# The diagonal of the recurrences' score tiles: from GpSimd's selects to VectorE's predicated copies

## The chip, the cores and the metric

One core of a Trainium2 chip runs the whole kernel. Its engines are TensorE (PE, and PEld for its weight loads), VectorE (DVE), ScalarE (ACT), GpSimd (POOL) and SyncE (SP, which issues most DMAs). The metric is the device time of one execution in microseconds (us): the median of three runs of the kernel before is 814.64 us (814.58 to 815.78).

## The reference

One layer: an input projection of x (1024 tokens by 1024 channels), three causal mixers side by side, a gated sum of their three up-projections, an output projection and a layer norm.

```
proj = x @ w_in
y_a  = stick-breaking attention(a_q, a_k, a_v) * silu(a_g)            # 4 heads
y_b  = rmsnorm(recurrence(h_q, h_key, h_i, log_f)) * silu(h_g)        # HGRN2: 4 heads, key width 64
y_c  = rmsnorm(recurrence(c_q, c_k, c_v, c_log_f)) * silu(c_g)        # GLA: 4 heads, key width 32
out  = layer_norm(alpha * x + (sum_n sigmoid(gate_n) * (y_n @ w_up[n])) @ w_out)

recurrence:  S_t = diag(f_t) S_(t-1) + k_t^T v_t ;  o_t = S_t^T q_t
```

In chunks, o_t has a part from the state in front of the chunk and a part `scores @ v` inside the chunk, where `scores[t, s] = sum_k q[t,k] * exp(cum[t,k] - cum[s,k]) * k[s,k]` for s <= t and 0 elsewhere. On the diagonal (s = t) the decay is 1, so the entry is q_t . k_t.

## The kernel before

TensorE is given the projections as a stream of generators (`stream`): each takes 128 or 256 columns of w_in, splits them into a rounded part and a rest (ScalarE's `copy` and VectorE's `subtract` in `split`, lines 98 and 99) and runs three matmuls per product. Five chains are woven into that stream: two of attention (`c_sb`), then three recurrences (`c_rec`): GLA with four heads at once (`nh == 4`), and HGRN2 twice with two heads each, called H0 and H1 below. A `yield` in a chain gives its time budget to the stream. A scheduler then places the instructions on each engine's queue; a queue runs in order.

`c_rec` treats windows of 128 tokens. Its score tiles `sc` are 128 by 1024 float32: four in GLA, two in H0, two in H1 (`nbank`). They, and GLA's query tiles `Qbd`, lie in six shared buffers (`S`, `NSLOT = 6`), which the attention's transposed weights `ath` and `atl` use before. In order:

1. Matmuls of products q*k with a block of ones (line 826) give `r`: per token, window and head the diagonal q_t . k_t in the first half and the neighbour's entry, `r1`, in the second (VectorE copies it out of PSUM on line 827).
2. GpSimd sets `Qbd` and `Qlo` to zero, and makes each `sc` by an `affine_select` (line 843): `r` on the diagonal, zero elsewhere.
3. The levels h = 1, 2, 4, ..., 64. From h = 2 on, `scores` copies blocks of Q to `Qbd` (ScalarE, line 857), in GLA GpSimd takes the rounding rest to `Qlo` (line 860, eight instructions for half a level), TensorE multiplies with K (line 876), and the result goes to blocks of `sc`: by VectorE's `copy_predicated` (line 885) up to h = 16, by ScalarE from h = 32 (lines 883 and 880). Then Q and K are multiplied by the decays G (lines 899 and 900, VectorE) and G is halved (line 902, GpSimd).
4. `neighbours` (line 850): VectorE copies `r1` to every second element of `sc` under a mask, one instruction of 128x512 per tile.
5. The transposes of K (line 912), the states: matmuls to PSUM (line 929, two buffers) and a serial chain on VectorE (lines 935 and 937); then the outputs (lines 949 and 951, which read `sc`).

Of the kernel before, what the change touches and what calls it, by code (L numbers as in the profile page):

```python
# [10 lines left out]
I32 = mybir.dt.int32  # L11
AF = mybir.ActivationFunctionType
ALU = mybir.AluOpType
# [3 lines left out]
P = 128  # L17
# [38 lines left out]
def hybrid_layer_kernel(ctx, tc, x, x_t, w_in, gla_gate_w2, gla_gate_b, hgrn_lb_logits,  # L56
                        hgrn_norm_g, gla_norm_g, w_up, w_out, ln_g, ln_b, out):
    nc = tc.nc
# [10 lines left out]
    def nm(s):  # L69
        cnt[0] += 1  # L70
        return f"{s}_{cnt[0]}"

    def S(name, dt=F32, shape=None):
        return sp.tile(shape or [P, 1024], dt, tag="s", name=nm(name), bufs=NS)
# [71 lines left out]
    ident = const.tile([P, P], F32, name="ident")  # L146
# [666 lines left out]
    def c_rec(key, nh, V):  # L813

        G, K, Q, pr = d[key]
        wpb = 8 // nh
# [4 lines left out]
        r = sm.tile([P, 16 * nh], F32, tag="r", name=nm("r"))  # L821
# [7 lines left out]
        sc = [S("sc", shape=[P, wpb, nh, P]) for _ in range(nbank)]  # L829
# [9 lines left out]
                nc.gpsimd.memset(q.bitcast(F32), 0.0)  # L839
            Khi, Klo = [[R("Kp", F32R) for _ in range(2)] for _ in range(2)]  # L840
        for b in range(nbank):
            rb = r[:, b * wpb * nh:(b + 1) * wpb * nh]
            nc.gpsimd.affine_select(sc[b].rearrange("p w h t -> p (w h) t"), rb.unsqueeze(2).broadcast_to([P, wpb * nh, P]),
                                    [[0, wpb * nh], [-1, P]], compare_op=ALU.is_equal, fill=0.0, base=0, channel_multiplier=1)
        yield R0_T if nh == 4 else R02_T
        def neighbours():

            for b in range(nbank):
                dst = sc[b].rearrange("p w a (n two) -> p (w a) n two", two=2)[:, :, :, 1]
                nc.vector.copy_predicated(dst, masks[1].bitcast(I32)[:, :, 0].unsqueeze(1).broadcast_to([P, wpb * nh, 64]),  # L850
                                          r1[:, b * wpb * nh:(b + 1) * wpb * nh].unsqueeze(2).broadcast_to([P, wpb * nh, 64]))
# [37 lines left out]
        for h in LEVELS:  # L889
            nb = 64 // h  # L890
            for hf in range(2):
# [11 lines left out]
                G[hf] = Gn  # L903
                yield R4_T if nh == 4 else R2_T
        neighbours()

        kn = []
# [35 lines left out]
        for b in range(nbank):  # L943
            pt = pav([P, wpb, nh, 64])
            for wi in range(wpb):
                w = b * wpb + wi
# [67 lines left out]
    def og_h(tt):  # L1014
        return [(d["og", ("H", un)][tt // 4][:, tt % 4].rearrange("p a v -> p (a v)"), P, un * P) for un in range(2)]

    chains = [(("qk", 0), lambda: c_sb(0)), (("qk", 1), lambda: c_sb(1)),
              ("GLA", lambda: c_rec("GLA", 4, lambda w: d["vC"][w // 2][:, w % 2, :])),
              (("H", 0), lambda: c_rec(("H", 0), 2, lambda w: d["vH"][0][w // 4][:, w % 4, :])),
              (("H", 1), lambda: c_rec(("H", 1), 2, lambda w: d["vH"][1][w // 4][:, w % 4, :]))]  # L1020
    for label, mk in chains:
        need(label)
# [22 lines left out]
    for tq in range(4):  # L1045
# [5 lines left out]
        for t2 in range(2):  # L1051
            tt = tq * 2 + t2
            np_ = 4 if tt == 7 else 2
            w = D // np_
# [4 lines left out]
            for i, cs in enumerate(cols):  # L1059
# [3 lines left out]
                for k in range(8):  # L1063
                    a, b = mh[k // 2][:, k % 2, t2 * P:(t2 + 1) * P], ml[k // 2][:, k % 2, t2 * P:(t2 + 1) * P]
# [69 lines left out]
```

## Time and profile before

| | before |
|---|---|
| median of 3 runs | 814.64 us |
| the profiled execution, whole | 814.49 us |
| its span, first to last instruction | 812.8 us |
| PE busy, DVE busy | 795.8 us (98%), 573.0 us (71%) |
| ACT busy, POOL busy | 369.3 us (45%), 183.3 us (23%) |
| mean granted TensorE clock | 0.997 of full |

Matmuls are pipelined, so a busy share of 98% does not mean that TensorE is at its peak; a wait in front of a matmul shows as idle time. The rows further down give the start of an instruction or of a run of equal ones (us from the span's start), its length in us, engine, line, operation, what it writes and reads, how many there are, and in brackets the idle time of its engine before it with what ended that.

### The profile page before, as it was taken

How to read it: one execution, taken by the hardware profiler on the slowest of the kernel's cores; microseconds unless marked ns; L12 is line 12 of the kernel's file. 1: busy time of each engine (PE TensorE's matmuls, PEld its weight loads, DVE VectorE, ACT ScalarE, POOL GpSimd, SP SyncE). 2: the span in 40 equal slices, each digit the busy share in tenths (PEclk: the TensorE clock that was granted, in tenths of full speed). 3: DMA queues.
4: the chain of work that ended last, by engine and by line, in shares of the span. 5: the costliest groups of instructions: out<-in, count | busy, mean ns of one | idle time of the engine just before them, and what ended most of it. 6: DMA issues, size and time to landing. Idle time of an engine off the chain costs nothing.

```text
span 812.8 us, 12525 instructions
## 1 busy us (share of the span) xinstructions
PE 795.8 (98%) x4504; PEld 681.0 (84%) x4504; DVE 573.0 (71%) x1058; ACT 369.3 (45%) x777; POOL 183.3 (23%) x358
## 2 busy tenths in 40 slices
PE   8999999999999999999999999999999999999996
PEld 6988799787779989988888889888888878888886
DVE  6449897869965497678665964766658566686675
ACT  6456565696644737454655433332224223341110
POOL 4012213122587822212110002112113121100000
PEclk9999999999999999999999999999999999999998
DMA  9533110111011111010111120220122202532221
GB/s 268 145 84 79 27 27 2 45 31 30 24 35 34 53 27 28 22 44 20 34 33 33 40 63 3 66 65 16 55 59 66 61 12 84 194 105 103 105 102 54
DMA packets 67790, 48.33 MB, mean 59 GB/s; under 512 B 4608, under 2 KB 61584, under 8 KB 67728
## 3 DMA queue, kind: packets, MB, share of 16 engines
q1 hardware_dynamic: 66288, 44.46, 19.8%
q10 hardware_dynamic: 1440, 3.08, 1.0%
q8 instruction: 35, 0.57, 0.3%
q14 instruction: 27, 0.22, 0.1%
HBM read 41.23 MB, written 4.19 MB: 56 GB/s over the span
## 4 chain that ended last, share of the span: by engine, by line
PE 80%; DVE 9%; POOL 4%; issue 3%; ACT 2%; DMA 1%; SPq 0%; POOLq 0%; DVEq 0%; ACTq 0%
PE mm L207 18%; PE mm L220 13%; PE z L621 13%; PE mm L1066 11%; PE tr L621 7%; PE mm L621 5%; PE z L876 4%; PE mm L504 2%; POOL Qlo L860 2%; DVE om L751 2%; PE av L951 1%; PE av L789 1%; DVE be L752 1%; PE tr L767 1%; DVE atl L99 1%
## 5 line engine op out<-in xcount | busy, mean ns | idle before, releaser
L207 PE MATMUL mm<-xh,wh 128*128 128x512 f32 x320 | 130.2, 407 | 0.0
L207 PE MATMUL mm<-xh,wl 128*128 128x512 f32 x320 | 127.0, 397 | 0.0
L207 PE MATMUL mm<-xl,wh 128*128 128x512 f32 x320 | 126.6, 396 | 0.0
L99 DVE TENSOR_TENSOR wl<-wr,wh 128x512 fp32r<-128x512 f32 (+3 forms) x116 | 80.7, 705 | 47.3 <-PE z L621 22.5
L98 ACT CAST wh<-wr 128x512 fp32r<-128x512 f32 (+3 forms) x116 | 64.6, 568 | 76.2 <-PE mm L207 33.4
L220 PE MATMUL mm<-wh,xh 128*128 128x256 f32 (+1 forms) x320 | 92.0, 288 | 0.3 <-ACT wh L98 0.2
L220 PE MATMUL mm<-wl,xh 128*128 128x256 f32 (+1 forms) x320 | 91.1, 285 | 0.5 <-DVE wl L99 0.4
L220 PE MATMUL mm<-wh,xl 128*128 128x256 f32 (+1 forms) x320 | 90.6, 283 | 0.1
L1066 PE MATMUL mm<-wo,mh 128*128 128x512 f32 (+1 forms) x288 | 80.7, 366 | 0.0
L207 PEld LDWEIGHTS mm<-xh,wl 128*128 128x128 f32 x320 | 60.1, 188 | 13.4
L207 PEld LDWEIGHTS mm<-xh,wh 128*128 128x128 f32 x320 | 60.7, 190 | 11.8 <-DVE mT L507 0.5
L207 PEld LDWEIGHTS mm<-xl,wh 128*128 128x128 f32 x320 | 60.5, 189 | 11.0
L220 PEld LDWEIGHTS mm<-wh,xh 128*128 128x128 f32 x320 | 60.5, 189 | 1.6 <-ACT wh L98 1.4
L220 PEld LDWEIGHTS mm<-wl,xh 128*128 128x128 f32 x320 | 60.4, 189 | 1.1 <-DVE wl L99 1.1
L220 PEld LDWEIGHTS mm<-wh,xl 128*128 128x128 f32 x320 | 60.5, 189 | 0.4 <-DVE xl L99 0.3
L1066 PEld LDWEIGHTS mm<-wo,mh 128*128 128x128 f32 x288 | 52.1, 189 | 8.7
L1066 PE MATMUL mm<-wo,ml 128*128 128x512 f32 (+1 forms) x144 | 52.8, 367 | 0.0
L860 POOL TENSOR_TENSOR Qlo<-Q,Qbd 32x128 fp32r<-32x128 f32 x96 | 48.2, 519 | 2.6
L747 POOL TENSOR_SCALAR_AFFINE_SELECT om<-om 128x128 f32<-128x128 f32 x32 | 12.7, 398 | 138.8 <-ACT om L742 133.3
L621 PE MATMUL mm<-yh,wu 128*128 128x512 f32 x128 | 42.4, 393 | 0.0
L621 PE MATMUL z<-xh,wh 128*128 128x512 f32 x104 | 41.7, 401 | 0.0
L621 PE MATMUL z<-xh,wl 128*128 128x512 f32 x104 | 41.2, 396 | 0.0
(258 smaller groups left out, 1808.6 us busy)
## 6 DMA issues: line engine op xcount, KB each, us to landing
wr<-in_w_in_dram SPq DMA_DIRECT2D x92, 256.0 KB, 3.1
xraw<-in_x_t_dram SPq DMA_DIRECT2D x16, 256.0 KB, 5.6
wr<-in_w_out_dram SPq DMA_DIRECT2D x16, 256.0 KB, 3.0
xr<-in_x_dram SPq DMA_DIRECT2D x8, 512.0 KB, 3.4
wr<-in_w_up_dram SPq DMA_DIRECT2D x24, 128.0 KB, 2.2
out_dram<-xr SPq DMA_DIRECT2D x7, 256.0 KB, 2.1
out_dram<-xr ACTq DMA_DIRECT2D x7, 256.0 KB, 2.0
ks<-ks SPq DMA_DIRECT2D x8, 128.0 KB, 2.2
```

Source lines behind the costliest of these rows:

```text
L98: nc.scalar.copy(hi, src)
L99: nc.vector.tensor_tensor(lo, src, hi.bitcast(F32), op=ALU.subtract)
L207: mm(pt, w_, x_, start=(n == 0), stop=(n == 23))
L220: mm(pt, x_, w_, start=(n == 0), stop=(n == 23))
L504: mm(pu, w_, y_[th], start=(k == 0), stop=(k == 5))
L621: mm(pt, w_, x_, start=(start and i == 0), stop=(stop and i == len(ops) - 1), skip_group_check=True)
L747: nc.gpsimd.affine_select(a_[:, cw - P:cw], a_[:, cw - P:cw], [[-1, P]], compare_op=ALU.is_gt, fill=fill, base=0, channel_multiplier=1)
L751: nc.vector.tensor_tensor_scan(rv, rv, rv, 1.0 if last else rt[:, 0:1], op0=ALU.mult, op1=ALU.bypass)
L752: nc.vector.tensor_tensor(be[:, 0:cw - 1], be[:, 0:cw - 1], om[:, 1:cw], op=ALU.mult)
L860: nc.gpsimd.tensor_tensor(Qlo[hf][i][rr, a, :].rearrange("p (n h) -> p n h", h=h), qo[rr, i * nb * 2:i * nb * 2 + nb * 2], Qbd[hf].bitcast ...
L876: mm(pt[:, wi * nh:(wi + 1) * nh], k_[:, w * P:(w + 1) * P], q.rearrange("p a (n h) -> p a n h", h=h), start=(n == 0 and wi == 0), stop=(n ...
L1066: mm(pt, l_, r_[e][:, o:o + w], start=(n == 0), stop=(n == 23))
```

## The change

`affine_select` from `r` becomes a `memset` to zero that reads nothing, at the same place. The diagonal is put in by a new `copy_predicated` in `neighbours`, in front of the old one: the mask is the 128x128 identity (its bits are non-zero on the diagonal), repeated for each window and head, the data is `r`, repeated along the row, and the target is the whole tile, 128x1024. There is one for each of the eight tiles.

```diff
         for b in range(nbank):
-            rb = r[:, b * wpb * nh:(b + 1) * wpb * nh]
-            nc.gpsimd.affine_select(sc[b].rearrange("p w h t -> p (w h) t"), rb.unsqueeze(2).broadcast_to([P, wpb * nh, P]),
-                                    [[0, wpb * nh], [-1, P]], compare_op=ALU.is_equal, fill=0.0, base=0, channel_multiplier=1)
+            nc.gpsimd.memset(sc[b], 0.0)
         yield R0_T if nh == 4 else R02_T
         def neighbours():
 
             for b in range(nbank):
+                n_ = wpb * nh
+                nc.vector.copy_predicated(sc[b].rearrange("p w h t -> p (w h) t"), ident.bitcast(I32).unsqueeze(1).broadcast_to([P, n_, P]),
+                                          r[:, b * n_:(b + 1) * n_].unsqueeze(2).broadcast_to([P, n_, P]))
                 dst = sc[b].rearrange("p w a (n two) -> p (w a) n two", two=2)[:, :, :, 1]
```

Lines behind the edit move by one (the old copy is on line 851 after it, 936 and 938 are the state's chain). GpSimd's queue at the start of GLA's recurrence, with the semaphores that each instruction waits for; `sc_2634` to `sc_2637` are the four score tiles. Before:

```order
L843 AFFINE_SELECT sc_2634<-r_2583 128x1024 [waits DVE_49,Activation_49]
L843 AFFINE_SELECT sc_2635<-r_2583 128x1024 [waits PE_49]
L839 MEMSET Qlo_2642 128x512
L839 MEMSET Qlo_2643 128x512
L839 MEMSET Qlo_2644 128x512
L839 MEMSET Qlo_2645 128x512
L843 AFFINE_SELECT sc_2636<-r_2583 128x1024 [waits PE_49,Activation_49]
L843 AFFINE_SELECT sc_2637<-r_2583 128x1024 [waits PE_49]
L860 TENSOR_TENSOR Qlo_2642<-Q_2356,Qbd_2638 32x128 [waits Activation_49,Pool_49]
```

And after:

```order
L842 MEMSET sc_2634 128x1024 [waits DVE_49,PE_49]
L842 MEMSET sc_2635 128x1024 [waits PE_49]
L842 MEMSET sc_2636 128x1024 [waits DVE_49,PE_49]
L839 MEMSET Qlo_2642 128x512
L839 MEMSET Qlo_2643 128x512
L839 MEMSET Qlo_2644 128x512
L839 MEMSET Qlo_2645 128x512
L842 MEMSET sc_2637 128x1024 [waits PE_49]
L861 TENSOR_TENSOR Qlo_2642<-Q_2356,Qbd_2638 32x128 [waits Activation_49,Pool_49]
```

The third tile's instruction moved ahead of the memsets of `Qlo`; its wait for PE is for the attention's last matmuls (line 789), which read that buffer. In H0 and H1 the memsets moved up on GpSimd's queue to the end of GLA's recurrence, ahead of the memsets of `Qbd`.

VectorE's queue at the end of GLA's levels: from the last step on K (line 900) to the state's chain (`St`); the lines 421 to 423 and 99 are work for the stream. Before:

```order
L900 TENSOR_TENSOR K_2175<-K_2175,G_3467 128x4x64
L421 SCALAR_TENSOR_TENSOR e_3489<-s_594_3487,s_595_3488 128x512
L850 COPY_PREDICATED sc_2634<-mask_78,r_2583 128x512
L422 SCALAR_TENSOR_TENSOR s_594_3487<-e_3489,lb,s_594_3487 128x512
L423 TENSOR_SCALAR s_595_3488<-s_595_3488,lb_126 128x512
L850 COPY_PREDICATED sc_2635<-mask_78,r_2583 128x512
L99 TENSOR_TENSOR wl_3811<-wr_3808,wh_3810 128x512
L850 COPY_PREDICATED sc_2636<-mask_78,r_2583 128x512
L850 COPY_PREDICATED sc_2637<-mask_78,r_2583 128x512
L99 TENSOR_TENSOR wl_3817<-wr_3814,wh_3816 128x512
```

And after, to the same point:

```order
L421 SCALAR_TENSOR_TENSOR e_3489<-s_594_3487,s_595_3488 128x512
L848 COPY_PREDICATED sc_2634<-ident,r_2583 128x1024
L422 SCALAR_TENSOR_TENSOR s_594_3487<-e_3489,lb,s_594_3487 128x512
L423 TENSOR_SCALAR s_595_3488<-s_595_3488,lb_126 128x512
L851 COPY_PREDICATED sc_2634<-mask_78,r_2583 128x512
L848 COPY_PREDICATED sc_2635<-ident,r_2583 128x1024
L99 TENSOR_TENSOR wl_3815<-wr_3812,wh_3814 128x512
L851 COPY_PREDICATED sc_2635<-mask_78,r_2583 128x512
L848 COPY_PREDICATED sc_2636<-ident,r_2583 128x1024
L848 COPY_PREDICATED sc_2637<-ident,r_2583 128x1024
L99 TENSOR_TENSOR wl_3821<-wr_3818,wh_3820 128x512
L851 COPY_PREDICATED sc_2636<-mask_78,r_2583 128x512
```

Four new copies stand among the old ones; behind these rows come, in both, lines 421 to 423 once more and then the state's chain (after the change with the last old copy among them).

VectorE's queue at the end of H0's levels, from the last step on the first half of K (`s_595`) to the state's chain. Before:

```order
L850 COPY_PREDICATED sc_3925<-mask_78,r_3874 128x512
L900 TENSOR_TENSOR s_605_3589<-s_605_3589,G_4395 128x4x64
L850 COPY_PREDICATED sc_3926<-mask_78,r_3874 128x512
L433 TENSOR_TENSOR Q_4476<-mm_4427,s_718_4294 128x512
L434 TENSOR_TENSOR prod_4477<-mm_4427,s_719_4295 128x512
L116 TENSOR_TENSOR prod_4484<-Q_4476,s_719_4295 128x256
L899 TENSOR_TENSOR Q_4476<-Q_4476,s_718_4294 128x256
L104 TENSOR_TENSOR prod_4477<-prod_4477,prod_4421 128x512
L900 TENSOR_TENSOR s_719_4295<-s_719_4295,s_718_4294 128x256
L935 COPY St_4516<-z_4520 64x64
L106 TENSOR_TENSOR prod_4423<-prod_4477,prod_4421 128x512
L104 TENSOR_TENSOR prod_4484<-prod_4484,prod_4424 128x256
```

And after:

```order
L848 COPY_PREDICATED sc_3929<-ident,r_3878 128x1024
L851 COPY_PREDICATED sc_3929<-mask_78,r_3878 128x512
L901 TENSOR_TENSOR s_605_3589<-s_605_3589,G_4399 128x4x64
L848 COPY_PREDICATED sc_3930<-ident,r_3878 128x1024
L433 TENSOR_TENSOR Q_4480<-mm_4431,s_718_4298 128x512
L434 TENSOR_TENSOR prod_4481<-mm_4431,s_719_4299 128x512
L116 TENSOR_TENSOR prod_4488<-Q_4480,s_719_4299 128x256
L851 COPY_PREDICATED sc_3930<-mask_78,r_3878 128x512
L104 TENSOR_TENSOR prod_4481<-prod_4481,prod_4425 128x512
L900 TENSOR_TENSOR Q_4480<-Q_4480,s_718_4298 128x256
L936 COPY St_4522<-z_4526 64x64 x2
L938 SCALAR_TENSOR_TENSOR St_4522<-St_4522,G_4454,z_4526 64x64
```

Two copies came in, and the state's two first copies now stand ahead of lines 106, 104 and the step on `s_719`. TensorE's queue is the same but for two matmuls of the stream that stand a few places earlier behind H0's states.

## Rows read from the trace of the kernel before

**Rows 1.** TensorE's waits: for whom, total us, times, longest
```profile
PE av L789 <- DVE atl L99: 3.2, 4, 1.4
PE z L876 <- DVE sc L885: 1.0, 3, 0.7
```

**Rows 2.** VectorE's waits
```profile
DVE Q L899 <- POOL Qlo L860: 25.5, 12, 2.7
```

**Rows 3.** Timeline, start of GLA's recurrence: start, us, engine, line, [idle before]
```profile
206.24 1.85 POOL L834 MEMSET Qbd<- 128x1024 f32 x2 [7.36 <-PE av L789]
...
214.11 2.65 POOL L843 TENSOR_SCALAR_AFFINE_SELECT sc<-r 128x1024 f32<-128x1024 f32 x2 [6.03 <-ACT Qbd L857]
...
215.46 0.28 PE L789 MATMUL av<-atl,V 128*128 128x256 f32 x1
...
215.73 1.30 DVE L899 TENSOR_TENSOR Q<-Q,f 128x256 f32<-128x256 f32 x1
...
216.71 1.92 POOL L839 MEMSET Qlo<- 128x512 f32 x4
...
216.96 0.41 DVE L900 TENSOR_TENSOR K<-K,f 128x256 f32<-128x256 f32 x1
...
218.59 2.61 POOL L843 TENSOR_SCALAR_AFFINE_SELECT sc<-r 128x1024 f32<-128x1024 f32 x2
...
221.17 9.66 POOL L860 TENSOR_TENSOR Qlo<-Q,Qbd 32x128 fp32r<-32x128 f32 x16
```

**Rows 4.** Timeline, GLA's level h = 2
```profile
231.65 2.45 DVE L885 COPY_PREDICATED sc<-mask,z 128x512 f32<-128x512 int32 x2
...
232.99 0.74 PE L876 MATMUL z<-Qbd,Kp 128*128 128x256 f32 x4 [0.66 <-DVE sc L885]
```

**Rows 5.** Timeline, GLA's level h = 16
```profile
267.81 1.34 DVE L885 COPY_PREDICATED sc<-mask,z 128x512 f32<-128x512 int32 x2
```

**Rows 6.** Timeline, end of GLA's levels and its states
```profile
284.77 1.33 DVE L850 COPY_PREDICATED sc<-mask,r 128x512 f32<-128x512 int32 x1
...
289.11 2.48 DVE L850 COPY_PREDICATED sc<-mask,r 128x512 f32<-128x512 int32 x2
...
293.40 0.48 DVE L423 TENSOR_SCALAR s<-s,lb 128x512 f32<-128x512 f32 x1
...
293.84 0.97 DVE L935 COPY St<-z 32x64 f32<-32x64 f32 x4
...
294.85 7.39 DVE L937 SCALAR_TENSOR_TENSOR St<-St,G,z 32x64 f32<-32x64 f32 x24
...
295.59 0.40 PE L207 MATMUL mm<-xh,wl 128*128 128x512 f32 x1
...
296.20 1.10 PE L929 MATMUL z<-vC,kn 128*128 128x256 f32 x4 [0.21 <-DVE St L937]
```

**Rows 7.** Timeline, end of H0's levels and its outputs
```profile
365.56 0.61 POOL L902 TENSOR_TENSOR G<-s 128x256 f32<-128x256 f32 x1 [4.25 <-DVE s L900]
365.61 1.74 DVE L850 COPY_PREDICATED sc<-mask,r 128x512 f32<-128x512 int32 x1 [0.19 <-ACT sc L880]
...
376.14 0.49 PE L949 MATMUL av<-St,Q 128*128 128x128 f32 x2 [0.35 <-DVE St L937]
```

**Rows 8.** Timeline, end of H1's levels
```profile
424.93 1.31 DVE L850 COPY_PREDICATED sc<-mask,r 128x512 f32<-128x512 int32 x1 [0.18 <-ACT sc L880]
...
430.32 0.69 DVE L507 TENSOR_TENSOR mT<-mm,gt 128x512 f32<-128x512 f32 x1 [1.78 <-PE mm L504]
```

**Rows 9.** Timeline, the start of the kernel
```profile
1.25 4.42 PE L1003 MATMUL z<-wz 128*128 128x512 bf16 x10 [1.25 <-DVE wz L145]
```

**Rows 10.** Timeline of TensorE, its last matmul
```profile
804.91 0.28 PE L1066 MATMUL mm<-wo,mh 128*128 128x256 f32 x1
```

**Rows 11.** Busy us and granted clock (0.91, 0.50) by stretch, the kernel's end
```profile
806.00:808.00 2.00, 0.00 (x0) 0.00 (x0) 1.90 (x8) 0.20 (x1) 0.00 (x0) 0.91 0.00 0
808.00:812.80 4.80, 0.00 (x0) 0.00 (x0) 1.10 (x2) 0.55 (x1) 1.50 (x2) 0.50 0.30 109
```

## The prediction

> **What bounds the kernel now.** I read the table of busy time first: PE 98%, DVE 71%, POOL 23%. TensorE works off its queue in order, and the end of the kernel is the end of that queue. So I read next for whom TensorE waits: the longest single waits for VectorE are 1.4 us (`atl`) and 0.7 us (`sc` in the levels, three times, 1.0 in all) [rows 1]. No wait there is for GpSimd. An edit on GpSimd or VectorE thus reaches the time only where it makes TensorE wait, or ends a wait. VectorE's waits say who sets the pace inside GLA's levels: 12 waits of together 25.5 us, all before line 899, for GpSimd's `Qlo` [rows 2]. VectorE has slack there, GpSimd has none. At the end of GLA's levels it is the other way round. The timeline shows VectorE's items one behind the other without an idle bracket; the state's first copies (line 935) start at 293.84 as line 423 ends (293.40 + 0.48), and at 296.20 TensorE's line 929 has waited 0.21 us for `St` [rows 6]. The z buffers are two, so the next states' matmuls can't start until the chain has read one: whatever is put on VectorE ahead of line 935 shows on TensorE nearly whole. I looked there, at the start of GLA, and at the same places in H0 and H1.
>
> **Step 1, GpSimd at the start of GLA: -1.6 us.** Before, four selects (2.65 + 2.61) and four memsets of `Qlo` (1.92) lead up to line 860, which starts at 221.17 [rows 3]. A memset of 128x1024 takes 1.85 / 2 = 0.93 [rows 3]. Taken alone that would be 5.26 - 3.7 = 1.6 less, and 6.03 us of idle time ahead of the first select [rows 3] seem to be there as well, since a memset doesn't wait for `r`. But the third memset now stands ahead of `Qlo`'s and waits for the attention's last matmul on line 789, which starts at 215.46 and lasts 0.28 [rows 3], so till 215.74. From there: third memset, `Qlo` 1.92, fourth memset 0.93, in all 215.74 + 0.93 + 1.92 + 0.93 = 219.5; with a start-up of 0.1, line 860 starts at 219.6 instead of 221.17. This gain is in the pacing chain, so I carry it to the end of the levels. Beside the selects, VectorE's 128x256 multiply on line 899 took 1.30, and the next one of that size 0.41 [rows 3]; this goes as well, but VectorE isn't the pace there. The bounds are 0 (TensorE has stream work to fill with, and moves no earlier) and -1.7.
>
> **Step 2, VectorE at the end of GLA: +4.2 us.** Four new copies of 128x1024. No row shows this one. Three rows are near. At h = 16, where the mask holds runs of 16, two predicated copies of 128x512 take 1.34 [rows 5]; at h = 2 two take 2.45 [rows 4]; line 850, which writes every second element, takes 1.33 alone and 2.48 for two [rows 6]. Line 850 reads its data from SBUF and costs what h = 2 costs with data from PSUM, so the place of the data isn't what doubles it; short runs in the operands are. The new copy writes a whole tile in order, reads the identity in order and repeats `r` along the row, which is nearest to h = 16: its 1024 elements as two instructions are 1.34, as one instruction some 1.25. In a row an instruction adds less than it lasts (line 850: 2.48 - 1.33 = 1.15 for the second), so I add 1.05 each, 4.2 for four. From below: a one-input 128x512 takes 0.48 [rows 6], twice 0.48 less a start some 0.8, added 0.6 each: 2.4. From above: the rate of line 850, two instructions of 512 or 2.48 for one of 1024, about 2.4 each: 9.6. There is no idle time on VectorE to take this up, and TensorE already waits at line 929, so all of it shows.
>
> In the rows two predicated elements side by side still cost double, and runs of 16 don't [rows 4, 5]. [...]
>
> **Step 3, TensorE's clock behind that wait: +1.6 us.** TensorE would stand at line 929 for 0.21 + 4.2, about 4.4 us in one piece, far longer than any wait before. After the last matmul (804.91 + 0.28) the granted clock averages 0.91 over 806 to 808 and 0.50 from 808 on [rows 10, 11]; a mean of 0.91 is 1.64 us at full and 0.36 at half, so it fell at about 807.6, 2.45 us after the matmul. The waits of 1.4 us left the clock where it was (mean 0.997). So I expect it to fall here. [...] If TensorE runs at half speed for as long behind the wait, some 4.4 us, 2.2 us of work are lost; about 0.6 of that falls in waits for the serial chain of line 937, which TensorE would have anyway. Bounds: 0 (it doesn't fall, or all is hidden) and 2.2.
>
> [...] Rows 11 show the fall only at the kernel's end; inside the kernel no row has a wait long enough.
>
> **Step 4, H0: +0.6 us.** Two copies, 2.1 more on VectorE ahead of the state's chain. Before, the first old copy ran beside GpSimd's line 902 and took 1.74 instead of 1.31 [rows 7, 8]; the new first copy meets that instead. VectorE's queue now has the state's first copies ahead of lines 106, 104 and the step on `s_719`, some 0.4 to 0.7 us each, which gives back about 1.5. The remaining 0.6 adds to the 0.35 that line 949 waits for `St` at 376.14 [rows 7]. Bounds: 0, and at the rate of line 850 some 2.7.
>
> **Step 5, H1: 0.** Two copies here too. VectorE then waits 1.78 us for TensorE before line 507 [rows 8], and with it the 2.1 us are covered but for 0.3 that the chain's own slack takes. At the slow rate 0.8 would show. The selects of H0 and H1 lay on GpSimd at places where nobody on TensorE waits: 0.
>
> **The sum.** 814.5 (the profiled execution, 0.15 below the median) - 1.6 + 4.2 + 1.6 + 0.6 = 819.3 us.
>
> **Rivals.**
> - The clock does not fall, because VectorE's order lets some matmuls of the stream into the gap: 814.5 - 1.6 + 4.2 + 0.6 = 817.7. For it: TensorE's queue has a stream matmul (line 207 at 295.59 [rows 6]) just ahead. Against it: the queue is in order and line 929 blocks what follows.
> - The copies cost what line 850 costs: four add 9.6 in GLA, H0 2.7, H1 0.8. That is 814.5 - 1.6 + 9.6 + 1.6 + 2.7 + 0.8 = 827.6; in GLA some of the 9.6 falls together with waits that are there anyway, so I say 827. For it: the only rows with line 850's operands [rows 6]; against it: runs of 16 at half that price [rows 5].
> - The copies are cheap (0.8 each, 2.4 in GLA), the clock stays up, H0 adds 0.2: 814.5 - 1.6 + 2.4 + 0.2 = 815.5. Little in the rows speaks for two-input copies at a one-input rate.
> - Faster: the selects' load on VectorE (line 899 at 1.30 instead of 0.41, and 1.6 us less on the pacing chain) is what delays TensorE, the 1.0 us of its waits in the levels [rows 1] go, and the copies fall into the time that VectorE wins: 814.5 - 1.6 - 1.0 + 0.6 = 812.5. It decides only if VectorE reaches line 935 earlier by more than the 4.2 us that the copies add. TensorE's waits for VectorE in the levels are small, so this has little room.
>
> **How the numbers follow.** Forecast 0.40, no clock fall 0.22, slow copies 0.18, cheap copies 0.13, faster 0.07. The forecast's own range is 818 to 821. Reaching from the cheap copies to just under the slow ones leaves out under 2 in 10: 815.0 to 826.0, as part of the slow case comes out lower, where H0 and the clock take less. A measurement of this kernel tells a change from none at about 0.2%, 1.6 us. Faster by more than that is 0.05 (part of the last rival); within it 0.15 (the cheap copies, the rest of the last rival); slower 0.80.
>
> **What would show it.** Step 1: line 861 starts at about 219.6. Step 2: each copy of line 848 lasts 1.25 us (2.5 for the slow rival, 0.8 for the cheap one), and TensorE waits 4.3 to 4.5 us for `St` at the states' matmul. Step 3: the granted clock of the stretch behind that wait is near 0.5 for some 4 us. Step 4: the wait before the outputs' matmul in H0 is near 1 us. Step 5: H1's stretch has its length of before. The prediction is wrong if that wait in GLA is under 2 us, or if TensorE waits at a place that I have not named.

## The result, and the profile after

The change makes the kernel slower: 821.42 us (median; 821.34 to 823.11) against 814.61 us, a ratio of 1.0086 (1.0074 to 1.0097). Forecast were 819.3 us and a range of 815.0 to 826.0. The profiled execution is the longest of its four, 823.11 us with a span of 821.4; the other three have spans of 819.6 or 819.7. Below, a time read from this one trace is held against the medians where the two differ.

TensorE's waits after the change (whom it waits for, total us, times, longest):

```profile
PE z L930 <- DVE St L938: 4.7, 1, 4.7
PE av L789 <- DVE atl L99: 3.2, 4, 1.4
...
PE av L950 <- DVE St L938: 0.7, 2, 0.5
...
PE mm L1067 <- DVE ml L99: 0.5, 1, 0.5
...
PE av L950 <- ACT og L955: 0.3, 1, 0.3
...
PE z L877 <- DVE sc L886: 0.2, 1, 0.2
```

The waits in the levels have gone from 1.0 us in three to 0.2 in one [rows 1], and one wait of 4.7 us stands at the top of the list, at the place where 0.21 stood [rows 6]. Two short waits, for `ml` near the end and for `og` in H0, stand where the kernel before had none in its list. GpSimd at the start of GLA's recurrence (start, us, engine, line, idle before):

```profile
212.06 1.85 POOL L842 MEMSET sc<- 128x1024 f32 x2 [3.51 <-PE av L789]
216.12 0.95 POOL L842 MEMSET sc<- 128x1024 f32 x1 [2.21 <-PE av L789]
217.01 1.93 POOL L839 MEMSET Qlo<- 128x512 f32 x4
218.88 0.96 POOL L842 MEMSET sc<- 128x1024 f32 x1
219.81 2.33 POOL L861 TENSOR_TENSOR Qlo<-Q,Qbd 32x128 fp32r<-32x128 f32 x4
```

`Qlo` begins at 219.81 instead of 221.17 [rows 3]. The idle time in front of the third memset is the wait for the attention's last matmul. VectorE at the end of GLA's levels:

```profile
283.54 1.33 DVE L848 COPY_PREDICATED sc<-ident,r 128x1024 f32<-128x1024 int32 x1
...
286.91 1.69 DVE L848 COPY_PREDICATED sc<-ident,r 128x1024 f32<-128x1024 int32 x1
...
290.20 2.56 DVE L848 COPY_PREDICATED sc<-ident,r 128x1024 f32<-128x1024 int32 x2
...
296.73 0.45 DVE L423 TENSOR_SCALAR s<-s,lb 128x512 f32<-128x512 f32 x1
297.11 0.96 DVE L936 COPY St<-z 32x64 f32<-32x64 f32 x4
```

A new copy takes 1.33 us alone, the price of line 850's copy of half the elements [rows 6]; two in a row take 2.56. The state's chain starts at 297.11, 3.3 us later than before, although VectorE reached the first copy of this stretch 1.2 us earlier (283.54 against 284.77 [rows 6]). TensorE there:

```profile
294.36 0.40 PE L207 MATMUL mm<-xh,wl 128*128 128x512 f32 x1
299.45 2.05 PE L930 MATMUL z<-vC,kn 128*128 128x256 f32 x4 [4.69 <-DVE St L938]
301.29 1.81 PE L952 MATMUL av<-vC,sc 128*128 128x64 f32 x8
...
306.27 0.78 PE L207 MATMUL mm<-xh,wh 128*128 128x512 f32 x1
```

The four matmuls behind the wait take 2.05 us; before they took 1.10 [rows 6]. The windows of this stretch say why (busy time of PE, PEld, DVE, ACT, POOL, each with its count, then the granted clock, DMA share, GB/s):

```profile
296.00:298.00 2.00, 0.00 (x0) 0.00 (x0) 1.91 (x7) 0.00 (x0) 0.78 (x1) 0.80 0.00 0
298.00:300.00 2.00, 0.55 (x1) 0.50 (x2) 1.77 (x8) 0.00 (x0) 0.00 (x0) 0.50 0.00 0
...
304.00:306.00 2.00, 2.00 (x10) 1.82 (x9) 1.15 (x5) 0.00 (x0) 0.00 (x0) 0.50 0.00 0
306.00:308.00 2.00, 2.00 (x8) 1.73 (x8) 0.21 (x1) 1.22 (x2) 1.31 (x2) 0.64 0.00 0
```

A mean of 0.80 over 2 us is 0.8 us at half, one of 0.64 is 1.44 us: the clock was at half from about 297.2 to about 307.4, 2.2 us inside the wait and 8.0 us behind it.

### The profile page after: what moved, and what is told of

The parts are those of the page before. It is cut to its first block, busy times and chain, and to the rows that moved or that the text cites. A ratio compares the mean times of both kernels' runs of the same rounds, so it can differ in the third digit from the quotient of the medians.

```text
span 821.4 us, 12528 instructions
## 1 busy us (share of the span) xinstructions
PE 799.7 (97%) x4504; PEld 685.0 (83%) x4504; DVE 578.2 (70%) x1066; ACT 369.6 (45%) x777; POOL 182.7 (22%) x358
## 4 chain that ended last, share of the span: by engine, by line
PE 78%; DVE 10%; POOL 3%; issue 3%; ACT 2%; DMA 2%; SPq 0%; POOLq 0%; DVEq 0%; ACTq 0%
PE mm L207 18%; PE mm L220 13%; PE z L621 12%; PE mm L1067 10%; PE tr L621 6%; PE mm L621 5%; PE z L877 4%; PE mm L504 2%; POOL Qlo L861 2%; PE av L789 2%; PE av L952 2%; DVE om L751 2%; PE tr L767 1%; DVE be L752 1%; DVE sc L848 1%
## 5 line engine op out<-in xcount | busy, mean ns | idle before, releaser
L99 DVE TENSOR_TENSOR wl<-wr,wh 128x512 fp32r<-128x512 f32 (+3 forms) x116 | 78.9, 689 | 49.4 <-ACT wh L98 23.5
```

Source lines behind the costliest of these rows:

```text
L99: nc.vector.tensor_tensor(lo, src, hi.bitcast(F32), op=ALU.subtract)
```

## The experiments

Each was run beside the kernel before, whose median then was 814.77 to 814.95 us. Diffs are against the change unless another kernel is named.

**1. The memsets alone.** The new copies are taken out; nothing writes the diagonal.

```diff
-                nc.vector.copy_predicated(sc[b]..., ident..., r...)
```

> Leaves out the diagonal of the score tiles in all three recurrences: the memsets stand as in the change, the eight new copies are gone. Theory (the loss is the copies' own time ahead of the state's chain and the clock behind it; the memsets alone gain): line 861's first run starts at about 219.8, TensorE's waits in the levels are near 0.2 as with the change, the wait for St before the third state tile is under 0.5 us, the clock stays at 1.00 inside the kernel, and the time is 814.6 - 1.5 = 813.1. Rival (the memsets' new place on GpSimd's queue carries part of the loss): over 815.

Measured: 813.21 us, ratio 0.9979 (0.9970 to 0.9988), 11 executions. The waits in the levels are down to 0.2 us, as with the change, and the wait for `St` is that of the kernel before, 0.21 us, 1.49 us earlier in time:

```profile
294.71 1.10 PE L927 MATMUL z<-vC,kn 128*128 128x256 f32 x4 [0.21 <-DVE St L935]
```

So step 1 is a gain of 1.7 us, and all of the loss hangs on the copies.

**2. The copies alone.** The selects stay, the copies are added.

```diff
-            nc.gpsimd.memset(sc[b], 0.0)
+            nc.gpsimd.affine_select(...)        # as before
```

> Keeps the selects of before on GpSimd and adds the eight copies of the change behind the levels (they write the same values again). Theory: the loss without step 1's gain, 821.4 + 1.5 = 822.9, with the wait for St before the third state tile still 4.2 to 4.8 us. Rival (GpSimd's gain does not reach the end of the levels, and the levels' shift in the trace is chance): 821.4, the same as the change.

Measured: 822.66 us, ratio 1.0093 (1.0080 to 1.0106). The gain of step 1 and the loss add up within the noise: 7.7 less 1.7 is 6.0, the change loses 6.8, and each ratio is known to about 1 us. Its wait and its clock:

```profile
300.81 2.04 PE L932 MATMUL z<-vC,kn 128*128 128x256 f32 x4 [4.76 <-DVE St L940]
...
306.38 0.48 PE L207 MATMUL mm<-xh,wh 128*128 128x512 f32 x1
```

```profile
298.00:300.00 2.00, 0.00 (x0) 0.00 (x0) 1.84 (x8) 0.00 (x0) 0.78 (x1) 0.56 0.00 0
...
304.00:306.00 2.00, 2.00 (x12) 1.83 (x11) 1.61 (x7) 0.00 (x0) 0.00 (x0) 0.73 0.00 0
306.00:308.00 2.00, 2.00 (x13) 1.75 (x12) 0.94 (x4) 1.22 (x2) 0.40 (x1) 1.00 0.00 0
```

The wait is that of the change (4.76 and 4.69). But here the clock is back at about 305.1, 4.3 us behind the wait's end, and the stretch up to line 207 lasts 5.57 us; in the change's profile it lasts 6.82 (299.45 to 306.27). A wait of the same length thus has a second part of its price that varies.

**3. The clock kept up.** Matmuls on zeros stand on TensorE's queue ahead of the third state tile, 14 of them and, in a second kernel, 20.

```diff
         for b in range(nbank):
+            if nh == 4 and b == 2:
+                keep = ptr([P, 512])
+                for i in range(14):             # 20 in the second kernel
+                    mm(keep, wz[:, 0:P], wz, start=True, stop=True)
```

> The change, and on TensorE 14 matmuls of 512 columns on zeros into an unused PSUM tile, ahead of the third state tile's matmuls, so that about 3.1 of the 4.7 us wait are filled with work that nobody reads. Theory (the clock's fall is a term of its own, 1.9 us in the median run, 3.6 in the profiled one): the granted clock stays at 1.00 behind the wait, the remaining wait is 1.2 to 1.7 us, and the time is 819.0 to 819.6. Rival (the serial chain of line 938 sets the pace behind the wait, so that the half clock costs nothing): 821.4.

> As the kernel with 14 matmuls on zeros in the wait, with 20 of them: about 4.6 us, the whole wait. Theory (with 14 the clock fell in four of six executions, since 1.7 and 1.4 us of idle time were left; the time without a fall is 820.1, of which 1.3 come from the states' matmuls now standing ahead of the outputs'): with the first wait filled the clock stays at full in every execution, and all lie at 819.8 to 820.6. Rival (what separates 820 from 824 is not the clock but chance elsewhere): the times still fall into two groups.

Measured with 14: a median of 823.70 us; two executions at 819.89 and 820.34 us with a mean clock of 0.998 and 0.997, four at 823.49 to 824.32 with 0.993 or 0.992. Neither the theory (819.0 to 819.6) nor the rival (821.4) had this. Measured with 20: 820.13 us, all five from 819.39 to 821.12, all with 0.997 to 0.999. So the clock is a term by itself, and filling the whole wait removes it; with the clock up the times still spread over 1.7 us. TensorE with 20 (the trace has a record of 19):

```profile
294.67 4.49 PE L931 MATMUL tr<-wz 128*128 128x512 bf16 x19
299.66 1.10 PE L935 MATMUL z<-vC,kn 128*128 128x256 f32 x4 [0.50 <-DVE St L943]
302.13 0.67 PE L935 MATMUL z<-vC,kn 128*128 128x256 f32 x2 [1.37 <-DVE St L943]
```

The four matmuls take 1.10 us again. The second wait, 1.37, is new: with the extra matmuls the scheduler put the fourth state tile ahead of the first outputs, which had filled this time. Without it these kernels would be near 818.8, by an estimate (820.13 less 1.37). The 14 left waits of 1.70 and 1.37 us in the one trace that there is, of an execution whose clock stayed up (820.34); by the mean clock it fell in the other group, four of six, but where it fell was not seen.

**4. Half the copies.** Only GLA's third and fourth tile get their diagonal.

```diff
+                if nh == 4 and b >= 2:
                     nc.vector.copy_predicated(sc[b]..., ident..., r...)
```

> The memsets of the change; of the eight copies only two of GLA's are left, those of the third and fourth tile, at the change's place. The diagonal is left out of GLA's other two tiles and of H0's and H1's. Theory (each copy adds 1.23 us to the wait for St before the third state tile, on from none without copies): a wait of 2.1 to 2.5 us; the clock has no cause to fall at half of the change's wait, so 813.2 + 2.3 = 815.5. Rival (the clock falls in this wait too): 817 to 818.5, with a granted clock near 0.5 behind the wait.

Measured: 816.21 us, 11 executions in groups: three at 814.66 to 814.91 (clock 0.997 to 0.999), seven at 815.57 to 816.81 (0.995 or 0.996 in six, 0.998 in one), one at 818.01 (0.993). My theory expected no fall and 815.5; by the mean clock seven of the 11 have one, of which one was traced. The rival had the fall, but at 817 to 818.5 only one execution. A mean clock of 0.995 is a hint and no proof, since single executions without a long wait have it too (816.51 in experiment 6, 815.46 in experiment 7); and the three under 815 lie below both forecasts, which stays open. The profiled one (816.81), its wait and then its clock:

```profile
296.68 1.64 PE L931 MATMUL z<-vC,kn 128*128 128x256 f32 x4 [2.59 <-DVE St L939]
```

```profile
294.00:296.00 2.00, 0.09 (x1) 0.00 (x0) 1.81 (x9) 0.00 (x0) 0.79 (x1) 1.00 0.41 119
296.00:298.00 2.00, 1.32 (x4) 1.14 (x5) 1.81 (x7) 0.00 (x0) 0.00 (x0) 0.78 0.00 0
298.00:300.00 2.00, 2.00 (x10) 1.91 (x10) 1.77 (x8) 0.00 (x0) 0.40 (x1) 0.50 0.00 0
300.00:302.00 2.00, 2.00 (x13) 1.83 (x13) 1.81 (x7) 0.00 (x0) 0.00 (x0) 0.87 0.00 0
```

A mean of 0.78 is 0.88 us at half: the clock fell at about 297.1, after TensorE had begun to work again at 296.68.

**5. GLA alone, H0 and H1 alone.** The branch on `nh` keeps the select for the others.

```diff
+            if nh == 4:                         # nh == 2 in the second kernel
                 nc.gpsimd.memset(sc[b], 0.0)
+            else: affine_select(...)            # as before
...
+                if nh == 4:                     # nh == 2 in the second kernel
                     nc.vector.copy_predicated(sc[b]..., ident..., r...)
```

> The change in GLA alone; H0 and H1 keep their selects and have no copies of the diagonal. Theory (the parts add: H0's cost 0.9 by itself): 821.4 - 0.9 = 820.5, with the wait for St before the third state tile at 4.6 to 4.8 us, the clock at half behind it, and line 949's waits in H0 back at 0.4. Rival (the parts share one delay): 821.4 or 819.5.

> GLA as before; memsets and copies only in H0 and H1. Theory (H0 costs what the trace of the change shows there, and H1 nothing): 814.7 + 1.1 = 815.8, with line 949's waits for St in H0 at 0.7 in all instead of 0.4, and no fall of the clock. Rival (H0's loss is a late effect of GLA's wait, which shifts the stream's work against the chains): 814.7, as before.

Measured: GLA alone 820.71 us, ratio 1.0068 (1.0056 to 1.0081); H0 and H1 alone 815.89, ratio 1.0012 (1.0003 to 1.0021). The first is a loss of 5.9 against the kernel before, the second of 0.9, and together they are the change's 6.8. The first trace has the wait of 4.7 us, the half clock behind it and H0's wait at 0.4; the second has no fall, and 0.7 in two in H0.

**6. The copies inside the levels.** In GLA one copy at the end of each half level h = 4 and h = 8, in H0 and H1 at h = 4; `diagonal(b)` is the change's copy for tile b.

```diff
-                nc.vector.copy_predicated(sc[b]..., ident..., r...)     # in neighbours
...
                 G[hf] = Gn
+                if nh == 4 and h in (4, 8): diagonal((h // 8) * 2 + hf)
+                elif nh == 2 and h == 4: diagonal(hf)
                 yield R4_T if nh == 4 else R2_T
```

> The copies of the diagonal are moved from behind the levels into them: in GLA one each at the end of the four half levels h = 4 and h = 8, in H0 and H1 one at each half of h = 4. Theory (the copies cost only where they stand ahead of the state's chain; in the levels VectorE waits up to 2.7 us at a time for Qlo): 814.6 - 1.5 = 813.1, the wait for St back at 0.2 to 0.5 us, clock 1.00 inside the kernel. Rival (beside a copy GpSimd's Qlo gets slower, and Qlo sets the pace: four times 0.4 to 1.2 us): 814.5 to 818.

Measured: 815.66 us, ratio 1.0008 (0.9999 to 1.0016): the wait of 4.7 us is gone, the clock stays at full in its trace, and yet it is 2.4 us above the memsets alone. The rival holds. All of `Qlo` (first here, then in experiment 1; busy us, mean ns):

```profile
L863 POOL TENSOR_TENSOR Qlo<-Q,Qbd 32x128 fp32r<-32x128 f32 x96 | 52.1, 560 | 2.7
```

```profile
L858 POOL TENSOR_TENSOR Qlo<-Q,Qbd 32x128 fp32r<-32x128 f32 x96 | 48.4, 521 | 2.6
```

That is 3.7 us more for four copies beside it. One of the places, both engines:

```profile
258.65 0.86 POOL L863 TENSOR_TENSOR Qlo<-Q,Qbd 32x128 fp32r<-32x128 f32 x2
258.26 1.30 DVE L888 COPY_PREDICATED sc<-mask,z 128x512 f32<-128x512 int32 x2
259.57 1.96 POOL L863 TENSOR_TENSOR Qlo<-Q,Qbd 32x128 fp32r<-32x128 f32 x2
259.60 1.65 DVE L846 COPY_PREDICATED sc<-ident,r 128x1024 f32<-128x1024 int32 x1
```

Line 888 is a copy of the level, line 846 the new one. The two `Qlo` instructions beside line 888 take 0.86 us, the next two, beside line 846, 1.96; in experiment 1 the first two of the same eight take 0.87, also beside a copy of the level:

```profile
256.73 0.87 POOL L858 TENSOR_TENSOR Qlo<-Q,Qbd 32x128 fp32r<-32x128 f32 x2
```

The copy itself takes 1.65 instead of 1.33. As `Qlo` paces the levels, TensorE's waits for `sc` rise to 1.4 us in four. The new copy has mask and data in SBUF, and the two `Qlo` instructions beside it take 1.96 us. The level's copies have their data in PSUM, and beside them `Qlo` keeps its pace: 0.86 for two, where the mean of one is 0.52 in experiment 1. Whether the place of the data or the size of the copy (128x1024 against 128x512) makes this difference is not shown.

**7. Another engine.** Against the kernel before: GLA's third and fourth tile are made by ScalarE, as the identity times `r`.

```diff
-        for b in range(nbank):                  # the selects
+        for b in range(2):
...
                     scores(h, hf, qo)
+                if h == 2 and hf == 0:
+                    for j in range(2 * wpb * nh, nbank * wpb * nh):
+                        w, a = j // nh, j % nh
+                        nc.scalar.activation(sc[w // wpb][:, w % wpb, a, :], ident, AF.Copy, scale=r[:, j:j + 1])
```

(In H0 and H1 the range is empty, and both tiles keep their selects.)

> The kernel before, with one edit: GLA's third and fourth score tile are made by ScalarE, 16 activations of 128x128 that multiply the identity by r (a scale per partition), behind the first half of level h = 2; the other selects stay on GpSimd, and nothing is added to VectorE. Theory (what the change gains is the shorter way to Qlo on GpSimd; here it is had without VectorE): line 860's first run starts at 218.7 to 219.7 instead of 221.2, TensorE's waits for sc in the levels are near 0.2, and the time is 813.0 to 813.5. Rival (ScalarE's 16 activations, some 4 us, delay Qbd and Kp, and TensorE waits for those): 814.7 or more.

Measured: 814.05 us, ratio 0.9989 (0.9981 to 0.9998). It beats both kernels, if by 0.9 us only, and lies between the theory's 813.5 and the rival's 814.7. ScalarE's 16 activations took 5.2 us in its trace, not some 4. GpSimd:

```profile
218.79 1.76 POOL L860 TENSOR_TENSOR Qlo<-Q,Qbd 32x128 fp32r<-32x128 f32 x3
...
225.08 4.23 POOL L860 TENSOR_TENSOR Qlo<-Q,Qbd 32x128 fp32r<-32x128 f32 x8
```

With three tiles by ScalarE:

> As the kernel with two tiles made by ScalarE, with three: 24 activations behind the first half of level h = 2, one select left on GpSimd in GLA. Theory (what can be gained at this place is TensorE's waits in the levels, 1.0 us, and those are gone with two tiles): line 860's first run starts some 1.3 us earlier, at about 217.5, and the time stays at 813.8 to 814.4. Rival (each microsecond on GpSimd's way to Qlo is one of the kernel's time): 812.8.

> As the kernel with three tiles made by ScalarE, but the second tile's eight activations now stand ahead of level h = 2, which writes into that tile. Theory (what can be gained at this place is TensorE's 1.0 us of waits in the levels, and those are gone with two tiles): line 860's first run starts at about 217.3, and the time stays at 813.8 to 814.4, or a little over where ScalarE's queue delays Qbd and Kp. Rival (each microsecond on GpSimd's way to Qlo is one of the kernel's time): 812.7.

The first of these doesn't answer the question: it has the second tile's activations behind level h = 2, which writes into that tile; what the level wrote is lost there, and its 818.21 us are those of another order of the work. The second gave 814.39 us, ratio 0.9992 (0.9983 to 1.0001), with `Qlo` from 217.58 on: 1.2 us more at the start of GpSimd's way, and nothing on the kernel. That does not decide between theory and rival, because the head start is gone within level h = 2. The last eight `Qlo` of that level with three tiles by ScalarE, and then its last twelve in experiment 1 (GLA's levels begin 0.2 us later in these traces than in that of the kernel before):

```profile
226.09 3.73 POOL L866 TENSOR_TENSOR Qlo<-Q,Qbd 32x128 fp32r<-32x128 f32 x8 [1.87 <-ACT Qbd L863]
```

```profile
221.97 7.34 POOL L858 TENSOR_TENSOR Qlo<-Q,Qbd 32x128 fp32r<-32x128 f32 x12
```

They end at 229.82 with three tiles, where GpSimd first waits 1.87 us for ScalarE's copy to `Qbd`, at 229.31 with two (225.08 + 4.23) and at 229.31 in experiment 1. So ScalarE's extra work takes back what GpSimd had gained: the delay of `Qbd` that the rival of the kernel with two tiles had named. Why that kernel still falls 0.8 us short of experiment 1's gain of 1.7 was not followed up.

**8. The change once more.**

> The changed kernel itself, more executions beside the kernel before. Theory (the wait of 4.7 us and H0's 0.9 are the same each time, the length of the half clock is not): executions with a mean clock of 0.994 at about 821.4, with 0.991 to 0.992 one to two us above, none under 820.5. Rival (the 1.7 us between the profiled run and the others came from the profiler or from the start): the clock does not go with the time.

Measured: 821.70 us, ratio 1.0082 (1.0068 to 1.0097). With the first four, nine executions:

| mean clock | times, us |
|---|---|
| 0.996 | 820.16, 820.70 |
| 0.994 | 821.34, 821.36, 821.48, 821.70 |
| 0.991 to 0.992 | 822.56, 823.11, 823.43 |

One lies below the 820.5 that I had set as the least, and neither of the two at 0.996 was foreseen; that the time goes with the clock holds. But the mean clock counts every fall. In the profiled execution, the one of 823.43, it fell at the kernel's start too:

```profile
8.00:10.00 2.00, 1.67 (x9) 1.26 (x10) 1.78 (x3) 1.42 (x4) 0.57 (x2) 0.98 1.18 294
10.00:12.00 2.00, 2.00 (x11) 2.00 (x11) 1.57 (x3) 1.43 (x3) 0.00 (x0) 0.50 1.18 290
12.00:14.00 2.00, 2.00 (x14) 2.00 (x13) 1.58 (x4) 1.60 (x4) 0.00 (x0) 0.67 1.18 291
```

From about 9.9 to 13.3 it was at half, and from there on TensorE runs 1.5 us later than in the trace of the kernel before (0.5 in the change's first profile). So the rival is right for about 1 us of this execution. The rest is the wait and the clock behind it, which is at half up to 306.9, 6.2 us behind the wait's end:

```profile
300.68 2.05 PE L930 MATMUL z<-vC,kn 128*128 128x256 f32 x4 [4.83 <-DVE St L938]
```

```profile
306.00:308.00 2.00, 2.00 (x13) 1.86 (x12) 1.11 (x4) 0.58 (x1) 0.49 (x1) 0.78 0.00 0
```

## Why the prediction was right, and where a size was off

| step | predicted | measured | from |
|---|---|---|---|
| 1, GpSimd in GLA | -1.6 | -1.7 | experiment 1 |
| 2, the copies before the state's chain | +4.2 | +4.5 | wait 0.21 to 4.69 |
| 3, the clock | +1.6 | 1.8 to 3.6 | below |
| 4 and 5, H0 and H1 | +0.6 | +0.9 | experiment 5 |

The sum came out 2.1 us low. The 821.42 us lie inside the range of 815.0 to 826.0, and 0.4 us above the forecast's own range of 818 to 821.

**Step 1** is right, including the reason why it is not 6 us: the wait for the attention's last matmul. In experiment 1's trace TensorE enters GLA's levels 0.2 us later than in the trace of before and leaves them 1.5 us earlier: 1.7 us won, of which the listed waits are 0.8 (1.0 before, 0.2 there). Experiment 7 wins 0.9 and 0.5 us by the medians; where its head start goes is shown there. The start-up of 0.1 us in the step's sum was an allowance that no row shows: in the change's trace line 861 starts 3.64 us behind the attention's last matmul (215.89 + 0.28 to 219.81), where the three durations of the sum alone are 3.78.

**Step 2** is right in place, mechanism and price. The copy is one of long runs (1.33, estimated 1.25), the slow rival (2.5) and the cheap one (0.8) are out. VectorE had no idle time to hide it, and TensorE's wait grew by what was put there, 4.5 us for four copies, 1.1 each where 1.05 was taken; the wait itself, 4.69, lies a little above the 4.3 to 4.5 named.

**Step 3** is the term that was mis-sized. The clock does fall, and experiment 3 shows the fall to be a cost of its own. I took 4.4 us at half speed, as long as the wait, and let 0.6 of the 2.2 us lost be hidden. No row of the kernel before shows the half speed behind a wait, nor the 0.6; in the change's trace the clock is at 0.50 there, and four matmuls take 2.05 us instead of 1.10 [rows 6]. A trace gives the price when it is held against the kernel before: by how much TensorE's delay grows from the last line 207 in front of the wait (295.59 [rows 6]) to a matmul behind the half clock, less what the wait itself grew from its 0.21. This is that later matmul before, in the change's first and second profile, and with the copies alone:

```profile
302.85 0.59 PE L949 MATMUL av<-St,Q 128*128 128x256 f32 x2
```

```profile
309.69 0.59 PE L950 MATMUL av<-St,Q 128*128 128x256 f32 x2
```

```profile
310.08 0.59 PE L950 MATMUL av<-St,Q 128*128 128x256 f32 x2
```

```profile
309.23 0.59 PE L952 MATMUL av<-St,Q 128*128 128x256 f32 x2
```

| trace | us at half while TensorE works | half of it | the delay grows by | less the wait's growth |
|---|---|---|---|---|
| half the copies | 3.4 | 1.7 | 3.75 | 1.4 |
| the copies alone | 4.3 | 2.1 | 6.3 | 1.8 |
| the change in GLA alone | 4.7 | 2.4 | 6.5 | 2.0 |
| the change, second profile | 6.2 | 3.1 | 7.4 | 2.8 |
| the change, first profile | 8.0 | 4.0 | 8.1 | 3.6 |

The price is each time half of the time at half clock less 0.3 to 0.4 us. So the shape of the step holds, and the hidden part is 0.3 to 0.4 and not 0.6. Its length is what failed: no row said how long the clock stays down, "as long as the wait" was a guess, and it was near in two traces. Two profiles of one program differ by 1.8 us in it; what sets it stays open.

From the medians: 814.6 - 1.7 + 4.5 + 0.9 = 818.3, which leaves 3.1 us to 821.4, and 2.6 by the estimate of experiment 3 (818.8). These are what is left over, and hold whatever else was not counted. The wait for `ml` may be a part: it is 0.5 us in the change's profile and 0.7 in that of H0 and H1 alone, and none in that of the kernel before.

**Step 4** was 0.3 low. The first new copy in H0 runs beside GpSimd's line 903, as foreseen, and takes the 1.74 us that the old one had taken there [rows 7]:

```profile
372.43 1.74 DVE L848 COPY_PREDICATED sc<-ident,r 128x1024 f32<-128x1024 int32 x1 [0.19 <-ACT sc L881]
```

The wait before line 950 went from 0.35 to 0.7 in two, where near 1 us was named, and 0.3 came in for `og`; the rest was not followed up. **Step 5** holds in the trace: behind H0 TensorE's delay against the kernel before stays as it is through H1.

The prices that steps 4 and 5 give for slow copies, 2.7 and 0.8, don't follow from their figures: two copies of 2.4 less the 1.5 given back are 3.3, less the 1.78 of H1's wait 3.0. As the copies were not slow, only that rival's 827 hangs on it.

The prediction also called itself wrong if TensorE waited at a place that it had not named. The waits for `og` and `ml`, 0.8 us together, are such places; the one that carries the loss was named.

The largest part of the 2.1 us between 819.3 and the median is step 3. Without a fall of the clock, where a rival had put the time at 817.7, the kernel would be at 818.3 to 818.8, by the two estimates above.

## What to carry to other kernels

An engine with slack on average need not have it where the work lands: VectorE was 71% busy overall, and without a gap in front of the serial chain that TensorE waits for. Where it did have gaps, in the levels, the copies slowed GpSimd instead, which sets the pace there (2.4 us in experiment 6). A wait of some microseconds on a full TensorE can cost twice, once as itself and once in the clock behind it: here 4.7 us and another 1.8 to 3.6, so the second belongs in a forecast as a range. And a head start on the pacing engine counts only if it lasts: what experiment 7 won at the start of the levels was gone before level h = 2 was through, because ScalarE, which had taken over the work, then kept GpSimd waiting (1.87 us with three tiles).

## What was not expected of the hardware

The clock fell with a wait of 2.59 us, and only after TensorE was working again (one trace; seven of 11 executions of that kernel by their mean clock). By the mean clock it fell in four of six executions of a kernel whose trace has waits of 1.70 and 1.37 us close together. In the traces of the kernel before and of the change the single waits of 1.4 us for `atl` did not drop it. In another trace it fell at 9.9 us, in a stretch (8 to 10 us) in which TensorE was idle for 0.33 us in all. After waits of 4.7 to 4.8 us it was back 4.3, 4.7, 6.2 and 8.0 us later in four traces, of which the last two are of one program. VectorE's copy of the diagonal, with mask and data in SBUF, held up GpSimd by 1.1 us: 1.96 for two instructions that take 0.86 beside a copy with its data in PSUM.
